# A feed-forward layer's gate and up products as seven half-size products in place of eight

## The chip, the cores and the metric

The kernel runs on one core of a Trainium2 chip. The metric is the device time of one execution in microseconds (us). Three runs of the kernel before took 2739.49, 2741.16 and 2741.25 us; the median is 2741.16 us. The engines are named as in the profile: PE is TensorE's matmul, PEld its load of the stationary operand, DVE is VectorE, ACT is ScalarE, POOL is GpSimd, and SP issues the transfers (DMAs).

## The reference

It is one decoder block on 512 tokens, with a width of 2048 and an inner width of 5632, in float32. An attention part and a pooling part are mixed, projected and added to x. The change lies behind that, in the gated feed-forward:

```python
        x = x + mixed @ w_out[l]

        h2 = rmsnorm(x, ffn_norm_g[l])
        x = x + (jax.nn.silu(h2 @ w_ffn_gate[l]) * (h2 @ w_ffn_up[l])) @ w_ffn_down[l]
```

## The kernel before, in words

Everything is kept feature-major: a tile is 128 features on the partitions and 512 tokens along the columns. The weights are the stationary operand (128 x 128), the activations stream past them. To keep float32's precision each operand x is split into h = float32r(x) and l = float32r(x - h), and each product becomes three matmuls that add up in one bank of PSUM (`mm3`, L192): h.h, h.l, l.h. `split` (L168) makes h with a cast on ACT and l with a subtraction on DVE that reads x and h.

Each stage is a list of items for PE. `Program.emit` (L97) issues them in order and puts the loads and splits of the weights ahead of them: three raw buffers of 128 x 1024 (`raw`), which SP fills with 512 KB each, and five split buffers (`wsp`) of 512 columns. PE's order is the order written; on the other engines a scheduler orders the instructions.

`gemm` (L199) computes four column tiles at once, in four banks, over all row tiles. The stages around the change are these. The output projection has four such groups (L990); their `post` (L999) adds x, keeps x2 in SBUF and sums its squares. Then the inner width is walked in four chunks of 6, 6, 6 and 4 groups (L1033). A group (L1056) multiplies two column tiles of gate and two of up by the 16 tiles of the normed x2 (`make_h2`, L1008), that is 16 x 4 x 3 = 192 matmuls of 512 columns; its `post` (L1044) multiplies by the norm's factor for each token (`inv2_bc`), applies Silu, multiplies gate by up, and splits the result. Behind each chunk the down projection adds its part onto x2 (L1060). The last chunk stores the result.

Two pieces of other stages serve as a measure of the change's operations. The attention's projections (`k_item`, `v_item`, L737 and L764) have matmuls of 256 columns, and the norms of the attention's heads run on POOL (`norm_chain`, L656, and L760).

Of the kernel before, what the change touches and what calls it, by code (L numbers as in the profile page):

```python
# [10 lines left out]

# [13 lines left out]
NT = S // 128  # L25
# [5 lines left out]
FF_CHUNKS = (6, 6, 6, 4)  # L31
# [9 lines left out]
RAW_BUFS, WSP_BUFS = 3, 5  # L41
WARM = 8
# [3 lines left out]
class Unit:  # L46
    """A stretch of weights that one DMA brings: n columns of float32 per partition, used in pieces."""
# [19 lines left out]
class Step:  # L67
    """Work other than a piece's that an item needs done ahead of it."""
# [5 lines left out]
class Program:  # L74
    """Tensor-engine items in issue order; the weights of later items are split ahead of them."""
# [4 lines left out]
    def item(self, run, pieces=(), post=(), pre=()):  # L80
        """post: (delay in items, function); pre: (lead in items, function)"""
# [48 lines left out]
def hybrid_block(ctx, tc, xT, pos, wcq, wckv, wkr, wu, wgp, wga, wgrp, wpo, wq, wkv, wao, wo,  # L130
                 wgu, wdn, vec, rgain, ident_d, mask_d, freq_d, cnt_d, out):
# [6 lines left out]
    stage = ctx.enter_context(tc.tile_pool(name="stage", bufs=1))  # L138
    work = ctx.enter_context(tc.tile_pool(name="work", bufs=1))
    dram = ctx.enter_context(tc.tile_pool(name="dram", bufs=1, space=bass.MemoryType.DRAM))  # L140
    psum = ctx.enter_context(tc.tile_pool(name="psum", bufs=2, space=bass.MemoryType.PSUM))
    SETS = ("aacc", "bbcd")
# [25 lines left out]
    def split(hi, lo, src, scale=None):  # L168
        """hi + lo = src (times a factor per partition), hi on ScalarE, lo on VectorE."""
# [22 lines left out]
    def mm3(o, w_h, w_l, a_h, a_l, start, stop):  # L192
        pe.matmul(o, w_h, a_h, start=start, stop=False)  # L193
        pe.matmul(o, w_h, a_l, start=False, stop=False)  # L194
        pe.matmul(o, w_l, a_h, start=False, stop=stop)  # L195
# [60 lines left out]
    def units_of(w, g, n):  # L256
        return [w[g, u] for u in range(n)]

# [1 line left out]
    vecs = small([128, N_VEC])  # L260
    nc.sync.dma_start(vecs, vec)
    ident = small([128, 128])
# [881 lines left out]
```

## Time and profile before

| | |
|---|---|
| median of 3 runs | 2741.16 us |
| span of the profiled execution | 2739.4 us |
| profiled execution's own device time | not given apart from its span; the three runs lie 0.1 to 1.9 us above it |
| PE busy | 2729.4 us, 100% of the span, 12712 matmuls |
| PEld busy | 2279.0 us |
| DVE, ACT, POOL busy | 1189.2, 940.0, 102.0 us |
| first matmul of gate and up | 1297.42 us after the span's start |
| DMA | 295.51 MB, mean 108 GB/s |

A group's row has the line, the engine, the operation, the output and the inputs by the program's names (buffer numbers left out), partitions x columns and the count; after the bar the busy time in us and the mean duration of one in ns, and after the next bar the idle time of the engine ahead of it and what ended it. A row of the timeline begins with the start and the duration in us. Matmuls overlap in the pipeline, so that the distance between two starts, not the duration, is what one costs. L-numbers are lines of the kernel that the row belongs to; those of the changed kernel are its own.

### The profile page before, as it was taken

To read this page: it belongs to the slowest core of one execution; us is meant where nothing else is said; L and a number is where in the kernel's file an instruction comes from. 1 tells how busy PE (TensorE), PEld (TensorE's weight loads), DVE (VectorE), ACT (ScalarE), POOL (GpSimd) and SP (SyncE) were. 2 spreads that over 40 slices of the span, in tenths; PEclk is the share of its full clock that TensorE was granted. 3 is DMA by queue.
4 is the path that set the end of the run, shared out by engine and by line. 5 is a ranking of instruction groups with operands and counts; after the bars stand their busy time and mean duration, and the time that the engine had idled before them with its cause. 6 is when DMAs were issued, how large, how long until landed. Compare 5 with 4: busy or idle time off the path is not lost.

```text
span 2739.4 us, 32926 instructions
## 1 busy us (share of the span) xinstructions
PE 2729.4 (100%) x12712; PEld 2279.0 (83%) x12712; DVE 1189.2 (43%) x2372; ACT 940.0 (34%) x1924; POOL 102.0 (4%) x232
## 2 busy tenths in 40 slices
PE   9999999999999999999999999999999999999999
PEld 7888888888888888888888888888888888888887
DVE  6555323367777644344333333333332333333343
ACT  5223223366667432233222322223222222222231
POOL 0000000021323000000000000000000000000000
PEclk9999999999999999999999999999999999999999
DMA  5223333322222554342232232322323222232233
GB/s 181 85 93 115 122 120 128 112 89 85 93 89 82 190 164 151 119 141 98 93 100 95 98 100 92 100 94 99 99 94 100 94 99 97 96 100 93 100 94 121
DMA packets 95085, 295.51 MB, mean 108 GB/s; under 512 B 10832, under 2 KB 11216, under 8 KB 94928
## 3 DMA queue, kind: packets, MB, share of 16 engines
q1 hardware_dynamic: 94928, 293.41, 32.6%
q8 instruction: 99, 1.62, 0.2%
q14 instruction: 58, 0.48, 0.1%
HBM read 272.40 MB, written 20.97 MB: 107 GB/s over the span
## 4 chain that ended last, share of the span: by engine, by line
PE 99%; DMA 0%; ACT 0%; SPq 0%; DVE 0%; issue 0%
PE psc L194 11%; PE psc L193 11%; PE psc L195 11%; PE psa L193 9%; PE psa L194 9%; PE psa L195 9%; PE psb L193 8%; PE psb L194 8%; PE psb L195 8%; PE psd L193 5%; PE psd L195 5%; PE psd L194 5%; PE psb L791 1%; PE psc L822 1%; PE psc L697 1%; PE psb L790 0%
## 5 line engine op out<-in xcount | busy, mean ns | idle before, releaser
L172 DVE TENSOR_TENSOR wsp<-raw,wsp 128x512 fp32r<-128x512 f32 (+1 forms) x954 | 649.7, 684 | 1413.3 <-ACT wsp L171 1410.9
L171 ACT CAST wsp<-raw 128x512 fp32r<-128x512 f32 (+1 forms) x954 | 587.7, 617 | 1612.5 <-PE psd L195 798.2
L195 PE MATMUL psc<-h,wsp 128*128 128x512 f32 x528 | 205.4, 389 | 0.0
L193 PE MATMUL psc<-h,wsp 128*128 128x512 f32 x528 | 205.4, 389 | 0.0
L194 PE MATMUL psc<-h,wsp 128*128 128x512 f32 x528 | 205.4, 389 | 0.0
L193 PE MATMUL psa<-h,wsp 128*128 128x512 f32 x352 | 137.4, 390 | 0.0
L195 PE MATMUL psa<-h,wsp 128*128 128x512 f32 x352 | 137.0, 389 | 0.0
L194 PE MATMUL psa<-h,wsp 128*128 128x512 f32 x352 | 136.9, 389 | 0.0
L193 PE MATMUL psb<-h,wsp 128*128 128x512 f32 x352 | 136.9, 389 | 0.0
L194 PE MATMUL psb<-h,wsp 128*128 128x512 f32 x352 | 136.9, 389 | 0.0
L195 PE MATMUL psb<-h,wsp 128*128 128x512 f32 x352 | 136.9, 389 | 0.0
L193 PE MATMUL psa<-wsp,lr 128*128 128x256 f32 (+1 forms) x384 | 120.9, 315 | 1.0 <-ACT pt L758 1.0
L194 PEld LDWEIGHTS psc<-h,wsp 128*128 128x128 f32 x528 | 99.1, 188 | 20.7
L195 PEld LDWEIGHTS psc<-h,wsp 128*128 128x128 f32 x528 | 99.1, 188 | 20.6
L193 PEld LDWEIGHTS psc<-h,wsp 128*128 128x128 f32 x528 | 99.0, 188 | 20.5
L195 PE MATMUL psa<-wsp,lr 128*128 128x256 f32 (+1 forms) x384 | 115.4, 300 | 0.0
L194 PE MATMUL psa<-wsp,lr 128*128 128x256 f32 (+1 forms) x384 | 115.3, 300 | 0.0
L193 PE MATMUL psc<-hT,wsp 128*128 128x512 f32 x288 | 112.6, 391 | 0.0
L195 PE MATMUL psc<-hT,wsp 128*128 128x512 f32 x288 | 112.6, 391 | 0.0
L194 PE MATMUL psc<-hT,wsp 128*128 128x512 f32 x288 | 112.5, 391 | 0.0
L193 PE MATMUL psc<-ff,wsp 128*128 128x512 f32 x264 | 102.7, 389 | 0.0
L194 PE MATMUL psc<-ff,wsp 128*128 128x512 f32 x264 | 102.7, 389 | 0.0
(309 smaller groups left out, 5619.8 us busy)
## 6 DMA issues: line engine op xcount, KB each, us to landing
raw<-in_wgu SPq DMA_DIRECT2D x176, 512.0 KB, 3.3
raw<-in_wdn SPq DMA_DIRECT2D x88, 512.0 KB, 3.3
raw<-in_wgp SPq DMA_DIRECT2D x32, 512.0 KB, 3.3
raw<-in_wga SPq DMA_DIRECT2D x32, 512.0 KB, 3.4
raw<-in_wao SPq DMA_DIRECT2D x32, 512.0 KB, 3.5
raw<-in_wo SPq DMA_DIRECT2D x32, 512.0 KB, 3.3
raw<-in_wu SPq DMA_DIRECT2D x16, 512.0 KB, 3.4
G_d<-tmp SPq DMA_DIRECT2D x32, 256.0 KB, 2.8
```

Of the source, the lines that this page charges most:

```text
L171: act.copy(out=hi, in_=src)
L172: dve.tensor_tensor(out=lo, in0=src, in1=hi.bitcast(F32), op=ALU.subtract)
L193: pe.matmul(o, w_h, a_h, start=start, stop=False)
L194: pe.matmul(o, w_h, a_l, start=False, stop=False)
L195: pe.matmul(o, w_l, a_h, start=False, stop=stop)
L697: pe.transpose(box[0][:, j * 128:(j + 1) * 128], src[t][:, j * 128:(j + 1) * 128], ident)
L791: pe.matmul(s[:, :w], P.QR[hp, h, q], P.KL[hp, :w], start=False, stop=True)
L822: pe.transpose(box[0][:, j * 128:(j + 1) * 128], P.st[h, i][:, j * 128:(j + 1) * 128], ident)
```

## The change

Gate and up are taken as one product of a 2 x 2 block matrix of weights and a 2 x 2 block matrix of activations. The weights' blocks are named by output (1 gate, 2 up) and half of the input width; so 11 and 12 are gate's halves, 21 and 22 up's. The activations' blocks are the same halves of the width by halves of the tokens (256 columns). A form of Strassen's identity (Winograd's) gets the four result blocks from seven block products in place of eight, with sums of blocks ahead of the products and behind them.

The activations' sums are made once, in the output projection (`operands`): for each pair of row tiles seven operands, split into h and l side by side, `T[i, j]`. The weights' sums are made for each of the 44 tiles of the inner width, in a class called `Macro`. A macro loads four blocks of 128 x 1024, makes four sums (two on POOL, two on DVE), splits seven operands of 1024 columns, and issues seven products of 8 x 3 matmuls with 256 columns, in the order 1, 6, 2, 7, 5, 4, 3. Product 2 adds onto product 1's bank. `post` adds the products up, applies the norm's factor (partly on POOL) and Silu, and stores the tile to DRAM (`F_d`).

The down projection runs after all macros, in two halves of 22 inner tiles, and reads its operands back from `F_d` (`make_act`). x2 goes to DRAM (`X2_d`), as does the sum after the first half (`X3_d`). The buffers of the three parts (ahead of the macros, macros, down) lie in pools that are closed and opened between the parts, in the same memory. The item list is emitted in two programs, with the macros between them.

```diff
-FF_CHUNKS = (6, 6, 6, 4)
+FT = D_FF // 128
+HT = FT // 2
+RAW2_BUFS, WS_BUFS = 6, 3
...
+        def sums():
+            t, b = box["t"], box["b"]
+            d, e = slot(F32, "d"), slot(F32, "e")
+            t1, t2, t3, t4 = d[:, :, LO], d[:, :, HI], e[:, :, LO], e[:, :, HI]
+            dve.tensor_tensor(out=t1, in0=t[:, :, HI], in1=t[:, :, LO], op=ALU.subtract)
+            dve.tensor_tensor(out=t2, in0=b[:, :, HI], in1=t1, op=ALU.subtract)
+            dve.tensor_tensor(out=t3, in0=b[:, :, HI], in1=t[:, :, HI], op=ALU.subtract)
+            dve.tensor_tensor(out=t4, in0=t2, in1=b[:, :, LO], op=ALU.subtract)
+            box.update({1: t[:, :, LO], 2: b[:, :, LO], 3: b[:, :, HI], 4: t4, 5: t1, 6: t2, 7: t3})
...
+    ORDER = (1, 6, 2, 7, 5, 4, 3)
+    TAGS = {1: "a", 6: "b", 7: "c", 5: "c", 4: "b", 3: "d"}
+    LEAD = 2
...
+        def split(self, i, src):
+            r = fast.tile([128, 2, 1024], F32R, name="ws", tag="ws", bufs=WS_BUFS)
+            split(r[:, 0, :], r[:, 1, :], src)
+            self.s[i] = r
+
+        def prepare(self, i):
+            raw = self.raw
+            if i == 1:
+                self.split(1, raw["11"])
+            elif i == 6:
+                self.s3 = fast.tile([128, 1024], F32, name="s3", tag="raw", bufs=RAW2_BUFS)
+                pool.tensor_tensor(out=self.s3, in0=raw["11"], in1=raw["21"], op=ALU.subtract)
+                pool.tensor_tensor(out=raw["21"], in0=raw["21"], in1=raw["22"], op=ALU.add)
+                dve.tensor_tensor(out=raw["11"], in0=raw["21"], in1=raw["11"], op=ALU.subtract)
+                self.split(6, raw["11"])
+            elif i == 2:
+                self.split(2, raw["12"])
+            elif i == 7:
+                self.split(7, self.s3)
+            elif i == 5:
+                self.split(5, raw["21"])
+            elif i == 4:
+                self.split(4, raw["22"])
+            else:
+                dve.tensor_tensor(out=raw["12"], in0=raw["12"], in1=raw["11"], op=ALU.subtract)
+                self.split(3, raw["12"])
+
+        def product(self, i):
+            if i == 2:
+                o = self.ps[1]
+            else:
+                o = self.ps[i] = ps(TAGS[i])[:, LO]
+            s = self.s[i]
+            for k in range(HK):
+                c = slice(k * 128, (k + 1) * 128)
+                t = T[i, k // 2][:, k % 2, :]
+                mm3(o, s[:, 0, c], s[:, 1, c], t[:, LO], t[:, HI], k == 0 and i != 2, k == HK - 1, onto=i == 2)
...
+            elif i == 4:
+                dve.tensor_tensor(out=self.gu[:, 1, LO], in0=self.u3, in1=o, op=ALU.subtract)
+                pool.tensor_tensor(out=self.gu[:, 1, :], in0=self.gu[:, 1, :], in1=inv2_bc, op=ALU.mult)
+            else:
+                g = self.gu
+                dve.tensor_tensor(out=g[:, 0, HI], in0=o, in1=self.u4, op=ALU.add)
+                pool.tensor_tensor(out=g[:, 0, HI], in0=g[:, 0, HI], in1=inv2_bc[:, HI], op=ALU.mult)
+                act.activation(out=g[:, 0, :], in_=g[:, 0, :], func=AF.Silu)
+                dve.tensor_tensor(out=g[:, 1, :], in0=g[:, 0, :], in1=g[:, 1, :], op=ALU.mult)
+                nc.sync.dma_start(F_d[self.f], g[:, 1, :])
```

How the instructions stand in the built programs follows here at three places. First DVE in the steady part of gate and up. Before, `post` of a group (`tmp`, `ff`) stands among splits of 512 columns:

```order
L172 TENSOR_TENSOR wsp<-raw,wsp 128x512 x16
L1049 TENSOR_TENSOR tmp<-psa,bc 128x512
L1051 TENSOR_TENSOR tmp<-psc,bc 128x512
L1049 TENSOR_TENSOR tmp<-psa,bc 128x512
L1052 TENSOR_TENSOR tmp<-tmp 128x512
L1051 TENSOR_TENSOR tmp<-psc,bc 128x512
```

Now DVE goes through one macro like this, from the split of product 3 to the first split for the next product 2 (`ws` are split buffers, `raw` the weights' blocks, `u` and `gu` the sums behind the products; `raw_15185` is this macro's block 12, `raw_15187` and `raw_15226` are the next one's blocks 11 and 21):

```order
L180 TENSOR_TENSOR ws_15348<-raw_15185,ws_15348 128x1024
L1160 TENSOR_TENSOR u_15376<-psc_15351,u_15286 128x256
L1161 TENSOR_TENSOR gu_15315<-psc_15351,u_15345 128x256
L180 TENSOR_TENSOR ws_15381<-raw_15187,ws_15381 128x1024
L1116 TENSOR_TENSOR raw_15187<-raw_15226,raw_15187 128x1024
L1163 TENSOR_TENSOR gu_15315<-u_15345,psb_15384 128x256
L180 TENSOR_TENSOR ws_15419<-raw_15187,ws_15419 128x1024
L1167 TENSOR_TENSOR gu_15315<-psd_15422,u_15376 128x256
L180 TENSOR_TENSOR ws_15454<-raw_15411,ws_15454 128x1024
```

The subtraction L1116 stands in DVE's queue ahead of the sum L1163 and of the splits of products 6 and 2; it reads what POOL has made.

POOL was idle in this part before, but for one operation of 4 columns. Its queue now, over the same macro (`s3` is the difference of 11 and 21, in a buffer of the raw ones):

```order
L1114 TENSOR_TENSOR s3_15415<-raw_15187,raw_15226 128x1024
L1115 TENSOR_TENSOR raw_15226<-raw_15226,raw_15379 128x1024
L1164 TENSOR_TENSOR gu_15315<-gu_15315,bc_111 128x512
L1168 TENSOR_TENSOR gu_15315<-gu_15315,bc_111 128x256
L1114 TENSOR_TENSOR s3_15641<-raw_15413,raw_15452 128x1024
```

The first of these waits for the split `ws_15348` of product 3, which frees its buffer; that split's cast waits for the last matmul of product 7. The second waits for the first.

Last, DVE where the output projection ends. Before, behind the last sum of x and x2 (L1001, `psd`) stood the squares and the splits of the normed x2, among splits of the weights:

```order
L1001 TENSOR_TENSOR x_11162<-psd,x_11162 128x512
L320 TENSOR_TENSOR s<-s,tmp 128x512
L172 TENSOR_TENSOR wsp<-raw,wsp 128x512
L320 TENSOR_TENSOR s<-s,tmp 128x512
L175 SCALAR_TENSOR_TENSOR h_11653<-x_11160,k_74,h_11653 128x512
```

Now the last group's sums and seven splits (`T`) stand there, and only then the first split of a macro's weights; ahead of these rows are the last sums of x and x2, the squares and the products with the norm's gain:

```order
L1020 TENSOR_TENSOR d_11542<-y_11536 128x2x256
L1022 TENSOR_TENSOR e_11543<-y_11539,y_11536 128x2x256
L1021 TENSOR_TENSOR d_11542<-y_11539,d_11542 128x2x256
L180 TENSOR_TENSOR T_11548<-y_11536,T_11548 128x2x256
L1023 TENSOR_TENSOR e_11543<-d_11542,y_11539 128x2x256
L180 TENSOR_TENSOR T_11551<-d_11542,T_11551 128x2x256
L180 TENSOR_TENSOR T_11554<-y_11539,T_11554 128x2x256
L180 TENSOR_TENSOR T_11557<-e_11543,T_11557 128x2x256
L180 TENSOR_TENSOR T_11560<-d_11542,T_11560 128x2x256
L180 TENSOR_TENSOR T_11563<-e_11543,T_11563 128x2x256
L180 TENSOR_TENSOR T_11566<-y_11539,T_11566 128x2x256
L180 TENSOR_TENSOR ws_11580<-raw_11574,ws_11580 128x1024
```

The macro's first split has moved behind all of the last group's operands, where before the weights' splits stood between them.

More of the change, by code (lines that the diff above doesn't have):

```diff
@@ L10 @@
 import math
+from contextlib import ExitStack
 import concourse.bass as bass
@@ L190, in split_piece, with mm3 @@
             split(p.t[:, 0, :p.n], p.t[:, 1, :p.n], raw)
[L192 to L195, printed above, removed]
+    def mm3(o, w_h, w_l, a_h, a_l, start, stop, onto=False):
+        for w, a, first, last in ((w_h, a_h, start, False), (w_h, a_l, False, False), (w_l, a_h, False, stop)):
+            pe.matmul(o, w, a, start=first, stop=last, skip_group_check=onto)
     prog = Program()
@@ L1073, in _turns @@
+    prog.emit(load_unit, split_piece, lambda load_next: None)
+    phase.close()
 def _turns(k):
```

235 lines of the change are left out of this document (164 added, 71 removed).

## The prediction

> **What bounds the kernel now.** I read the page's totals and its chain of waits first, then the table of stretches, then single rows.
>
> ```profile
> span 2739.4 us, 32926 instructions
> PE 2729.4 (100%) x12712; PEld 2279.0 (83%) x12712; DVE 1189.2 (43%) x2372; ACT 940.0 (34%) x1924; POOL 102.0 (4%) x232
> PE 99%; DMA 0%; ACT 0%; SPq 0%; DVE 0%; issue 0%
> ```
>
> TensorE (PE) is the bound: its matmuls fill the span and 99% of the chain. The stretches say whether this also holds where the change lies, in the feed-forward part (its first matmul starts at 1297.42, in a row below):
>
> ```profile
> core 0: us, PE busy (x) PEld busy (x) DVE busy (x) ACT busy (x) POOL busy (x), PEclk, DMA share, GB/s
> 1130.00:1305.00 175.00, 175.00 (x774) 144.91 (x773) 73.20 (x113) 57.93 (x97) 0.00 (x0) 1.00 0.35 116
> 1305.00:1600.00 295.00, 295.00 (x1305) 244.01 (x1304) 107.96 (x168) 83.11 (x133) 1.03 (x1) 1.00 0.30 97
> 1600.00:2000.00 400.00, 400.00 (x1767) 331.20 (x1766) 139.80 (x212) 106.35 (x171) 0.00 (x0) 1.00 0.30 96
> ```
>
> PE is busy for all of each stretch at full clock, while DVE (VectorE) and ACT (ScalarE) work a third of it, POOL (GpSimd) nearly nothing and the DMA engines 30%. So any matmul time saved here shows, as long as none of these others takes over. A busy PE isn't a rate, so the price of a matmul is the distance between starts:
>
> ```profile
> 2000.14 0.39 PE L195 MATMUL psc<-ff,wsp 128*128 128x512 f32 x1
> 2005.13 0.39 PE L193 MATMUL psc<-ff,wsp 128*128 128x512 f32 x1
> ...
> 626.86 0.28 PE L193 MATMUL psa<-wsp,lr 128*128 128x256 f32 x1
> 628.17 0.28 PE L195 MATMUL psa<-wsp,lr 128*128 128x256 f32 x1
> ```
>
> There are 22 distances between the first two rows (4.99 us): 0.2268 us for 512 columns. There are 11 between the last two (1.31 us): 0.119 us for 256 columns, each with weights of its own as in the change. Half the columns cost 5% more than half.
>
> **The matmuls.** Gate and up are 22 groups x 16 row tiles x 4 columns x 3 = 4224 matmuls of 512 columns: 4224 x 0.2268 = 958.0 us. The change has 44 macros x 7 products x 8 row tiles x 3 = 7392 of 256 columns: 7392 x 0.119 = 879.6 us. That is **-78 us**, not the eighth (-120 us) that the arithmetic promises. The down projection keeps its 2112 matmuls. A macro is 168 matmuls, 20.0 us, a product 2.86 us; a 44th part of gate and up was 21.8 us, so a stall of **1.8 us per macro** eats the gain.
>
> **What must be ready for a macro.** The sums of weights and the splits into high and low half move from 512 to 1024 columns and to more engines. Prices:
>
> ```profile
> L172 DVE TENSOR_TENSOR wsp<-raw,wsp 128x512 fp32r<-128x512 f32 x914 | 629.2, 690 | 1398.3 <-ACT wsp L171 1396.3
> L172 DVE TENSOR_TENSOR PT<-psc,PT 128x256 fp32r<-128x256 f32 x64 | 26.2, 419 | 24.1 <-ACT PT L171 24.1
> ...
> L171 ACT CAST wsp<-raw 128x512 fp32r<-128x512 f32 x914 | 568.0, 623 | 1594.4 <-PE psd L195 792.5 <-PE psc L195 772.3 <-issue 8.8
> L171 ACT CAST PT<-psc 128x256 fp32r<-128x256 f32 x64 | 23.8, 373 | 9.7 <-DVE PT L172 9.2 <-PE psc L822 0.5
> L1050 ACT ACTIVATE tmp<-tmp 128x512 f32<-128x512 f32 x44 | 27.9, 633 | 29.4 <-DVE tmp L1049 29.3
> ```
>
> 256 columns more cost DVE 271 ns and ACT 250 ns, so 1024 columns cost 690 + 2 x 271 = 1.23 us and 623 + 2 x 250 = 1.12 us. Per macro DVE has 9 of these (11.1 us), a product of 512 columns (0.69) and 8 sums of 256 (3.4): 15 us. ACT has 7 casts, a copy and a Silu: 8.9 us. Neither is the bound by itself. POOL gets two sums of 1024 columns and products of 512 and 256. Nothing like it stands in the trace; the nearest rows are small ones (minimum, median and maximum in ns):
>
> ```profile
> L658 POOL TENSOR_TENSOR ss<-ss,k x40: 194/195/554, 540.9 to 889.6; 128x2 f32<-128x2 f32 x32, 128x8 f32<-128x8 f32 x8
> L760 POOL TENSOR_SCALAR rt<-k,inv x64: 442/449/942, 546.1 to 892.2; 128x64 f32<-128x64 f32 x64
> ```
>
> (449 - 195) / 62 = 4.1 ns per column puts 1024 columns at 4.2 us, the dear end; the cheap end is DVE's 1.23 us for the same operation. I take the geometric middle, **2.3 us**, since the nearest POOL rows differ in operation and size. The Trainium skill (GPSIMD Engine Reference, 3.1) gives 4497 ns for such a sum over 2048 columns, which would make it about 2.25 us as an estimate from that page; no run here shows it.
>
> **Who shares with whom.** The long maxima in these rows have one cause, in this stretch of POOL and of DVE:
>
> ```profile
> 602.18 0.19 POOL L659 TENSOR_TENSOR ss<-ss,k 128x2 f32<-128x2 f32 x1
> 610.06 0.20 POOL L658 TENSOR_TENSOR ss<-ss,k 128x2 f32<-128x2 f32 x1 [2.58 <-ACT tmp L749]
> 614.34 0.47 POOL L658 TENSOR_TENSOR ss<-ss,k 128x2 f32<-128x2 f32 x1 [1.89 <-ACT tmp L749]
> 614.89 0.52 POOL L659 TENSOR_TENSOR ss<-ss,k 128x2 f32<-128x2 f32 x1
> ...
> 602.13 0.42 DVE L172 TENSOR_TENSOR PT<-psc,PT 128x256 fp32r<-128x256 f32 x1 [0.75 <-ACT PT L171]
> 614.08 1.28 DVE L172 TENSOR_TENSOR wsp<-raw,wsp 128x512 fp32r<-128x512 f32 x2
> ```
>
> Alone or beside a DVE operation that reads PSUM, POOL's op takes 0.19 to 0.20 us. Beside the two DVE subtractions with both inputs in SBUF it takes 0.47 and 0.52 us, and ends at 614.81 and 615.41: 0.05 us after the first subtraction (614.08 + 0.68) and after the pair (615.36). POOL stands still while DVE reads two SBUF operands. In the change DVE does this for 11.8 us of every macro, and POOL needs 2 x 2.3 + 1.2 + 0.6 = 6.4 us: 18 us of 20 that can't overlap.
>
> The Trainium skill (SBUF — State Buffer, "Who interferes with whom") says more than the rows: whichever starts first holds the port for its whole instruction and the other fully blocks. By that, DVE also waits out POOL's 2.3 us sums, worth a few us more over the span than if only POOL waits; the rows bear out one direction alone, since no POOL op here is long enough to hold DVE up.
>
> **The chain of a macro.** POOL's first sum (`s3`) needs a raw buffer, and the order of the program gives it the one that product 3's split frees. That split needs the split buffer that product 7 leaves. From product 7's end: last matmul's drain 0.16 (0.28 - 0.12), ACT cast 1.12, DVE split 1.23, POOL sum 2.3, the split for the next product 1, which sits between POOL's two sums on the shared reads, 1.23, POOL sum 2.3, DVE's subtraction that waits for it 1.23, ACT cast 1.12, DVE split behind POOL's product with the norm factor 0.4 + 1.23, and eight handoffs of 0.05 (0.08 from 614.81 to 614.89 on POOL): 12.7 us. There are four products (5, 4, 3 and the next 1), 11.4 us, until product 6 starts, plus 0.24 until its third matmul reads the low half: 11.7 us. It is **1.0 us late**.
>
> To that come a weight load that nothing hides, 0.19 us (the 188 ns below), and a knock-on between nothing and the Silu's 0.63 us, of which I take 0.4: product 2 adds onto product 1's bank and waits until ACT has copied it, and this copy stands behind the Silu, which waits for POOL's last product. 1.65 us x 43 = **+71 us**.
>
> ```profile
> L195 PEld LDWEIGHTS psc<-h,wsp 128*128 128x128 f32 x528 | 99.1, 188 | 20.6
> ```
>
> The stall's bounds: nothing at a POOL price under 1.8 us, or at 2.3 us if DVE's split didn't stand in the way (12.7 - 1.23 - 0.4 = 11.1 us); at 4.2 us the chain is 3.8 us longer and POOL's product some 0.5, 6 us per macro, +258 us.
>
> **The two seams.** Before, the output projection runs into the feed-forward without a gap:
>
> ```profile
> 1297.19 0.39 PE L195 MATMUL psd<-mixT,wsp 128*128 128x512 f32 x1
> 1297.42 0.39 PE L193 MATMUL psa<-h,wsp 128*128 128x512 f32 x1
> ...
> 1297.37 0.68 DVE L1001 TENSOR_TENSOR x<-psc,x 128x512 f32<-128x512 f32 x1
> 1297.96 0.68 DVE L320 TENSOR_TENSOR s<-s,tmp 128x512 f32<-128x512 f32 x1
> ...
> raw<-in_wgu SPq DMA_DIRECT2D x176, 512.0 KB, 3.3
> ```
>
> Now the weights' loads (3.3 us) stand on SP behind stores of x2 that wait for DVE, and some 17 DVE instructions for the last group of operands stand before the first macro's low half: 17 x 0.59 (the distance of the two DVE rows) + 1.23 = 11 us, and up to two POOL sums in between, 16 us. I take **+16**, as the rows above show such reads excluding each other. At the end of the macros the loads for down stand behind the last store of the product: drain 0.16, DVE 0.42, POOL 0.6, Silu 0.63, DVE 0.69, load 3.3, cast 0.62, handoffs: 7 us; with the splits of the first inner tiles queued on DVE and ACT ahead of these, up to 13. I take **+11**.
>
> The other operand groups (22 DVE instructions each, 13 us) lie in quarters of the output projection in which DVE is 42% busy (73.20 of 175); uncovered they would cost 3 x 13 us. The inner product's way through DRAM adds 88 transfers of 256 KB to queues at 30%: nothing.
>
> **Sum.** -78 + 71 + 16 + 11 = **+20 us**, onto the profiled execution's span of 2739.4; with the 1.8 us by which the median (2741.16) exceeds that span, **2761 us**. By the POOL price alone the case reaches from 2744 (2.1 us) to 2815 (2.8 us).
>
> **Rivals.**
> Macros without stall (0.38): POOL's sum costs under 1.8 us, or reads beside DVE when it streams long rows. For it: the rows show exclusion on ops of two columns only, and PE, DVE and ACT sums all stay below 20 us. Against: 18 of 20 us on one resource, in fixed order. -78 + 16 + 11 = -51: **2690 us**, at the cheap ends of the seams 2681.
> POOL as dear as its TENSOR_SCALAR row (0.05): 4.2 us a sum, stall 6 us per macro, slower from 2.1 us a sum on: -78 + 258 + 27 = +207, **2948 us**. Against it: that row has a scalar operand and a start-up of its own.
> Matmuls of 256 columns held to the 188 ns of a weight load: 7392 x 0.188 = 1390 us, +432, about 3173 us. The rows at 0.119 speak against it; under 0.01.
>
> **Numbers.** The forecast's case has 0.57: 0.50 slower and 0.07 where the stall is near 1.2 us and all cancels. 0.2% is 5.5 us, about what a measurement here can tell from no change. Faster 0.38, same 0.07, slower 0.50 + 0.05 = 0.55. The range runs from 2684 (no stall, seams near cheap) to 2830 (POOL near 3 us).
>
> **What would show it.** Right: in the macros PE waits for DVE's split of product 6 by about 1 us and for ACT's copy by a few tenths, POOL's 1024-column rows last over 2.3 us because DVE's reads hold them, macros come every 21 to 22 us, and PE pauses 10 to 20 us at each seam. Wrong: POOL's sums under 1.8 us, or macros every 20.0 us with PE waiting for nothing.

## The result and the profile after

The changed kernel takes 2775.17 us (median of 4 runs, 2772.37 to 2780.71), the kernel before 2740.67 beside it (2739.49 to 2741.25): a ratio of 1.0129, 95% interval 1.0114 to 1.0143. It is 1.3% slower; 2761 us had been forecast, in a range of 2684 to 2830. The profiled execution took 2773.10 us with a span of 2771.3.

The page's totals and its chain of waits, after:

```profile
span 2771.3 us, 40184 instructions
PE 2697.8 (97%) x15880; PEld 2393.0 (86%) x15880; DVE 1533.7 (55%) x2648; ACT 1046.6 (38%) x1936; POOL 483.9 (17%) x408
PE 18%; issue 1%; POOL 1%; ACT 1%; DMA 1%; DVE 0%; POOLq 0%; ACTq 0%; SPq 0%
```

PE's busy time fell only from 2729.4 to 2697.8 us, and 73.5 us of the span are now free of matmuls; before it was 10. The chain could be followed for a small part alone, so its shares say little here. The table of stretches says more:

```profile
core 0: us, PE busy (x) PEld busy (x) DVE busy (x) ACT busy (x) POOL busy (x), PEclk, DMA share, GB/s
900.00:1280.00 380.00, 379.55 (x1689) 313.09 (x1688) 185.04 (x320) 128.30 (x228) 0.00 (x0) 1.00 0.47 154
1280.00:1320.00 40.00, 25.37 (x112) 21.72 (x111) 20.86 (x30) 11.14 (x17) 8.85 (x2) 0.76 0.28 102
1320.00:1545.00 225.00, 206.76 (x1590) 201.93 (x1589) 153.47 (x174) 80.20 (x93) 78.36 (x37) 0.94 0.33 110
1545.00:2200.00 655.00, 636.35 (x5175) 623.77 (x5174) 456.53 (x524) 244.43 (x278) 267.15 (x124) 1.00 0.33 111
2200.00:2290.00 90.00, 75.85 (x604) 73.95 (x604) 73.01 (x94) 44.50 (x63) 28.55 (x14) 0.93 0.51 178
```

Ahead of the feed-forward PE is as full as before. At the first seam (1280 to 1320) it stands idle for 15 us of 40, and at the second (2200 to 2290) for 14 of 90. In the macros between them it waits a little in each. Two stretches of macros differ: up to 1545 PE is idle 8% of the time and the granted clock is 0.94; behind that it is 3% and 1.00.

The macros' stores of the inner product give their period: 24.24 us in the mean for the first eight intervals (193.9 us), 21.24 for the other 35 (743.5 us), most of them 21.27. The rows of one steady macro, PE first, then POOL and DVE (start, duration, and in brackets what ended the wait ahead):

```profile
1703.44 0.40 PE L203 MATMUL psb<-T,ws 128*128 128x256 f32 x2
1704.35 2.90 PE L203 MATMUL psb<-T,ws 128*128 128x256 f32 x22 [0.51 <-DVE ws L180]
1707.34 3.13 PE L203 MATMUL psa<-T,ws 128*128 128x256 f32 x24
1710.30 5.92 PE L203 MATMUL psc<-T,ws 128*128 128x256 f32 x48
1716.06 3.04 PE L203 MATMUL psb<-T,ws 128*128 128x256 f32 x24
1718.94 3.04 PE L203 MATMUL psd<-T,ws 128*128 128x256 f32 x24
...
1701.92 1.29 POOL L1164 TENSOR_TENSOR gu<-gu,bc 128x512 f32<-128x512 f32 x1 [1.67 <-DVE gu L1163]
1715.77 2.40 POOL L1114 TENSOR_TENSOR s<-raw 128x1024 f32<-128x1024 f32 x1 [9.41 <-DVE ws L180]
1718.25 3.27 POOL L1115 TENSOR_TENSOR raw<-raw 128x1024 f32<-128x1024 f32 x1
...
1702.70 1.59 DVE L180 TENSOR_TENSOR ws<-raw,ws 128x1024 fp32r<-128x1024 f32 x1 [0.86 <-ACT ws L179]
1710.27 1.21 DVE L180 TENSOR_TENSOR ws<-raw,ws 128x1024 fp32r<-128x1024 f32 x1
1717.35 1.90 DVE L180 TENSOR_TENSOR ws<-raw,ws 128x1024 fp32r<-128x1024 f32 x1 [0.33 <-ACT ws L179]
1721.55 1.23 DVE L1116 TENSOR_TENSOR raw<-raw 128x1024 f32<-128x1024 f32 x1 [2.29 <-POOL raw L1115]
```

Undisturbed products start 2.88 us apart (1716.06 to 1718.94): 0.120 us for a matmul, 20.16 us for the 168 of a macro. The 22 matmuls of product 6 (`psb`, 1704.35) start 0.67 us later than 1703.44 + 2 x 0.12, product 2 (1707.34) 0.35 later than their 22 x 0.12 allow, product 7 (1710.30) another 0.08. That is the stall of 1.10 us.

POOL's first sum takes 2.40 us though DVE's split starts beside it, as long as a sum with nothing beside it (2.37 at 1309.31, below). The DVE split that starts at 1717.35 takes 1.90 where others take 1.21: nearly all of its work lies behind POOL's end at 1718.17, and POOL's next sum, issued at 1718.25, in turn takes 0.87 more than 2.40. So DVE waits for POOL as POOL waits for DVE. The forecast's rows showed only the second; the rule of the Trainium skill (SBUF — State Buffer, "Who interferes with whom") that whichever starts first holds the port is borne out in both directions.

In the first eight intervals something else is added. The rows are ACT in the second of them, with one cast of the steady macro (1713.38) for comparison, then PE at the end of the first and of the second, and then the granted clock over the 22 matmuls of product 6 in both:

```profile
1375.66 0.62 ACT L179 CAST ff<-ff 128x512 fp32r<-128x512 f32 x1 [3.01 <-DMA ff<-F_d]
1376.18 2.23 ACT L179 CAST ws<-raw 128x1024 fp32r<-128x1024 f32 x2
...
1713.38 1.05 ACT L179 CAST ws<-raw 128x1024 fp32r<-128x1024 f32 x1 [1.83 <-PE psc L203]
...
1364.30 4.19 PE L203 MATMUL psb<-T,ws 128*128 128x256 f32 x22 [1.11 <-DVE ws L180]
1386.78 0.50 PE L203 MATMUL psb<-T,ws 128*128 128x256 f32 x2 [0.82 <-ACT ws L179]
1388.39 4.35 PE L203 MATMUL psb<-T,ws 128*128 128x256 f32 x22 [1.11 <-DVE ws L180]
1392.54 0.73 PE L203 MATMUL psa<-T,ws 128*128 128x256 f32 x4
```

```profile
1364.30:1368.29 3.99, 3.99 (x22) 3.99 (x23) 2.71 (x4) 1.83 (x3) 1.64 (x1) 0.64 0.00 0
1388.39:1392.54 4.15, 4.15 (x23) 4.15 (x23) 2.87 (x4) 1.83 (x3) 1.64 (x1) 0.61 0.00 2
```

The eight early reloads of the inner product (`ff<-F_d`), written for the last four macros, stand in the queues of the first eight: nothing held them back, since their buffers were free. Each is issued behind the store that it reads; its cast stands in ACT's queue and waits 3.01 us for it to land, and the casts of two weight splits stand behind it. The first of these belongs to product 3, whose split lets POOL's first sum begin. It starts 4.78 us behind product 7's start (1376.18, product 7 at 1371.40), in the steady macro 3.08 (1713.38 and 1710.30): 1.70 us later. Product 6's low half comes 2.35 us late in place of 0.67, 1.68 more. PE's waits there are 0.82 and 1.11 us, and then the granted clock drops: 22 matmuls take 4.15 us from start to start in place of 2.64. One wait of 0.51 us, in the steady macro, costs its length; these two cost 1.5 us more.

The seams, PE and POOL:

```profile
1293.85 0.84 PE L203 MATMUL psd<-mixT,wsp 128*128 128x512 f32 x3
1305.30 0.79 PE L203 MATMUL psa<-T,ws 128*128 128x256 f32 x2 [10.61 <-ACT ws L179]
1307.05 4.53 PE L203 MATMUL psa<-T,ws 128*128 128x256 f32 x22 [0.96 <-DVE ws L180]
1314.12 0.73 PE L203 MATMUL psb<-T,ws 128*128 128x256 f32 x2 [2.54 <-ACT ws L179]
1315.38 5.06 PE L203 MATMUL psb<-T,ws 128*128 128x256 f32 x22 [0.53 <-DVE ws L180]
1321.43 1.79 PE L203 MATMUL psa<-T,ws 128*128 128x256 f32 x13
2286.78 3.05 PE L203 MATMUL psa<-ff,wsp 128*128 128x512 f32 x6 [12.95 <-ACT wsp L179]
...
1302.74 6.49 POOL L1114 TENSOR_TENSOR s<-raw 128x1024 f32<-128x1024 f32 x1 [412.95 <-DMA raw<-in_wup]
1309.31 2.37 POOL L1115 TENSOR_TENSOR raw<-raw 128x1024 f32<-128x1024 f32 x1
```

POOL's first sum lasts 6.49 us under DVE's row of operand splits. The whole difference of the spans (31.9 us) then comes out like this:

| part | predicted | measured | how |
|---|---|---|---|
| matmuls of gate and up | -78 | -71.0 | 44 x 20.16 - 958.0 |
| eight intervals with a reload | 0 | +32.6 | 8 x (24.24 - 20.16) |
| the other 35 intervals | +71 with the eight | +37.9 | 743.5 - 35 x 20.16 |
| both seams' gaps | +27 | +34.7 | 2286.78 - 1294.53, less 937.4 between the first store and the last, less one macro |
| slow clock behind the second seam | 0 | +1.5 | six matmuls in 3.05 us, 1.52 elsewhere |
| part ahead | 0 | -2.9 | output projection ends at 1294.53 (1293.85 + 3 x 0.227), before at 1297.42 |
| sum | +20 | +32.8 | |

The first seam is 21 us of the 34.7 (1321.43 - 1294.53 - 2 x 2.88). Of the 32.6 us, 8 x 1.11 = 8.9 are the stall that the other intervals have too, and 23.8 are left for the reloads. The end of the output projection varies between runs by as much (it lies at 1297.70 in the run below with the operands behind the splits), so no cause is read from the -2.9 of the part ahead. About 1 us of the sum stays unassigned.

### The profile page after: what moved, and what is told of

It is laid out like the page before. It is cut to its first block, busy times and chain, and to the rows that moved or that the text cites. A ratio compares the mean times of both kernels' runs of the same rounds, so it can differ in the third digit from the quotient of the medians.

```text
span 2771.3 us, 40184 instructions
## 1 busy us (share of the span) xinstructions
PE 2697.8 (97%) x15880; PEld 2393.0 (86%) x15880; DVE 1533.7 (55%) x2648; ACT 1046.6 (38%) x1936; POOL 483.9 (17%) x408
## 5 line engine op out<-in xcount | busy, mean ns | idle before, releaser
L180 DVE TENSOR_TENSOR wsp<-raw,wsp 128x512 fp32r<-128x512 f32 (+1 forms) x602 | 406.2, 679 | 796.2 <-ACT wsp L179 791.8
L179 ACT CAST wsp<-raw 128x512 fp32r<-128x512 f32 (+1 forms) x602 | 368.3, 614 | 939.0 <-PE psd L203 456.7
L179 ACT CAST ws<-raw 128x1024 fp32r<-128x1024 f32 x264 | 272.4, 1049 | 459.2 <-DVE raw L1116 252.0
L180 DVE TENSOR_TENSOR ws<-raw,ws 128x1024 fp32r<-128x1024 f32 x264 | 377.8, 1431 | 77.7 <-ACT ws L179 77.5
L203 PE MATMUL psb<-T,ws 128*128 128x256 f32 x2112 | 291.7, 293 | 37.9 <-DVE ws L180 26.2
L203 PEld LDWEIGHTS psb<-T,ws 128*128 128x128 f32 x2112 | 273.3, 199 | 48.9 <-DVE ws L180 35.2
L203 PE MATMUL psa<-T,ws 128*128 128x256 f32 x2112 | 274.4, 286 | 14.9 <-ACT ws L179 10.6
L203 PEld LDWEIGHTS psa<-T,ws 128*128 128x128 f32 x2112 | 261.6, 193 | 23.3 <-ACT ws L179 11.0
L203 PE MATMUL psc<-T,ws 128*128 128x256 f32 x2112 | 260.6, 283 | 0.0
L203 PEld LDWEIGHTS psc<-T,ws 128*128 128x128 f32 x2112 | 256.6, 192 | 0.0
```

The costliest lines, as they stand in the source:

```text
L179: act.copy(out=hi, in_=src)
L180: dve.tensor_tensor(out=lo, in0=src, in1=hi.bitcast(F32), op=ALU.subtract)
L203: pe.matmul(o, w, a, start=first, stop=last, skip_group_check=onto)
```

## The experiments

All times are medians of at least 4 runs; the kernel before took 2740.1 to 2740.6 us beside them. A steady period is that of macros 10 to 37.

| edit to the changed kernel | steady period, us | time, us | ratio to before, interval |
|---|---|---|---|
| none | 21.27 | 2775.17 | 1.0129, 1.0114 to 1.0143 |
| sums on DVE | 20.16 | 2711.75 | 0.9896, 0.9882 to 0.9911 |
| reloads late | 21.27 | 2757.61 | 1.0063, 1.0048 to 1.0078 |
| both | 20.16 | 2706.07 | 0.9875, 0.9860 to 0.9890 |
| reloads late, both norm products on DVE | 20.56 | 2722.68 | 0.9941, 0.9924 to 0.9957 |
| reloads late, norm product of 512 columns on DVE | 20.90 | 2743.02 | 1.0009, 1.0000 to 1.0018 |
| reloads late, own buffer for the first sum | 19.8 to 20.95 | 2726.78 | 0.9947, 0.9932 to 0.9961 |
| both, down's weights early | 20.16 | 2691.67 | 0.9822, 0.9806 to 0.9839 |
| the same, operands behind the splits | 20.16 | 2691.68 | 0.9819, 0.9804 to 0.9834 |
| reloads late, chain longer by one operation | 21.84 | 2777.04 | 1.0135, 1.0118 to 1.0152 |
| reloads late, chain longer by two | 24.6 to 25.8 | 2888.12 | 1.0538, 1.0522 to 1.0554 |
| both, down's weights early, reloads one at a time | 20.16 | 2693.04 | 0.9827, 0.9812 to 0.9842 |
| the same, POOL idle | 20.16 | 2688.28 | 0.9811, 0.9794 to 0.9827 |

**Sums on DVE.**

```diff
-                pool.tensor_tensor(out=self.s3, in0=raw["11"], in1=raw["21"], op=ALU.subtract)
-                pool.tensor_tensor(out=raw["21"], in0=raw["21"], in1=raw["22"], op=ALU.add)
+                dve.tensor_tensor(out=self.s3, in0=raw["11"], in1=raw["21"], op=ALU.subtract)
+                dve.tensor_tensor(out=raw["21"], in0=raw["21"], in1=raw["22"], op=ALU.add)
```

> The two weight sums of a macro, 128 x 1024, go from POOL to DVE; the two products with the norm's factor stay on POOL. In the changed kernel a steady macro comes every 21.27 us, where its 168 matmuls alone need 168 x 0.120 = 20.16; the first nine come every 24.15. Theory A (POOL's sums, 2.40 alone and 3.27 us when DVE's reads hold them, make the macro late): DVE does each in 1.22 us, the chain loses 2.40 + 3.27 - 2 x 1.22 = 3.2 us and no longer waits, so steady macros come every 20.2 us, and the first nine too if the same chain sets them: 2775 - 37 - 36 = about 2702 us. If the first nine have a cause of their own (theory B: eight early reloads of the inner product stand in SP's queue ahead of the weights' loads), they stay at 23 to 24 us and the time is about 2738. Theory B for every macro (SP's queue with its store and loads sets the period): nothing changes, 2770 to 2778, or slower, as DVE gets 2.4 us more work per macro.

Measured 2711.75 us, 63 less. The steady period is 20.16: the chain without POOL's sums no longer reaches PE. The eight intervals with a reload take 21.1 us in the mean, so the reloads still cost about 1 us each, where 0 or 3 had been expected; with room in the chain they cost less, not nothing. (The expectation speaks of nine such macros; the stores show eight.)

**Reloads late.** Eight tiny copies keep the eight buffers taken until four macros before the end.

```diff
+        if i == 1 and m.f == 1:
+            pads = [slot(F32, "pad") for _ in range(8)]
+        if i == 1 and m.f in (1, FT - 4):
+            for r in pads:
+                dve.tensor_copy(r[:, 0, 0:1], m.raw["22"][:, 0:1])
```

> The eight reloads of the inner product that the scheduler had placed among the first eight macros (each behind the store that it reads, ahead of the next weights' loads in SP's queue) are held back until four macros before the end, by eight tiny copies that keep their buffers taken; sums stay on POOL. Theory B (the reloads delay the weights in the first nine macros): their period falls from 24.15 to the steady 21.3 us, 9 x 2.9 = 26 us, and the time to about 2749; the steady macros keep 21.27. Theory A alone (POOL's chain, made longer there by the granted clock of 0.91 to 0.95 and by the doubled DMA traffic): the first nine stay at 23.5 us or more and the time within 2768 to 2778.

Measured 2757.61 us. The early periods are 21.27 (the first 20.97), so the reloads were the whole difference of the eight intervals: 8 x (24.24 - 21.27) = 23.8 us. But the macros where they now stand took 26.66 and 21.82, which gives 5.9 back: 17.9 us are left, and 17.6 were measured. The expectation put the cause into SP's queue ahead of the weights' loads. SP's rows in the changed kernel, with a reload and without, don't show that:

```profile
1367.71 0.33 SPq L1171 DMA_DIRECT2D F_d<-gu  x1
1370.40 0.42 SPq L1087 DMA_DIRECT2D ff<-F_d  x1
1371.49 2.77 SPq L1100 DMA_DIRECT2D raw<-in_wg  x2
...
1707.78 0.33 SPq L1171 DMA_DIRECT2D F_d<-gu  x1
1711.55 1.76 SPq L1100 DMA_DIRECT2D raw<-in_wg  x2
```

From the store to the loads of gate it is 3.78 us in the one and 3.77 in the other. The second of the two loads is issued about 1 us later with a reload, but no operation between 1340 and 1545 waits for a load of weights: the waits for transfers there are the eight casts of reloads, 27.0 us, and one of 1.3 us for a store. The place that the rows show is ACT's queue, as above; no run moved the cast alone, so it is read from rows, not tried.

**Both.** The two edits together.

> Both edits: sums on DVE and reloads late. Theory A for the steady macros and B for the first nine, added up: every macro at 20.2 us, 2775 - 73 = about 2702 us, of which only the two seams (15 and 13 us) are left as gaps of PE; -71 + 28 against the kernel before = about 2698. If DVE, now with some 17.6 us of work in 20.2, becomes late itself (theory C: the work was moved, not removed), macros come at 20.5 to 21.5 us and the time is 2715 to 2760.

Measured 2706.07 us: 34.1 less than before, where 2702 had been expected by the sum of the theories. PE is busy in every microsecond from 1500 to 1800. DVE is 83% busy there (249 us of 300) and PE doesn't wait for it, so the theory that the work was only moved falls. POOL still makes its two products under DVE's reads:

```profile
1718.18 2.16 POOL L1164 TENSOR_TENSOR gu<-gu,bc 128x512 f32<-128x512 f32 x1 [17.24 <-DVE gu L1163]
1720.36 0.74 POOL L1168 TENSOR_TENSOR gu<-gu,bc 128x256 f32<-128x256 f32 x1
```

2.16 us in place of 1.29, and it costs nothing, since the chain ends early enough.

**Both norm products on DVE, then one.** The sums stay on POOL; the reloads are late.

```diff
-                pool.tensor_tensor(out=self.gu[:, 1, :], in0=self.gu[:, 1, :], in1=inv2_bc, op=ALU.mult)
+                dve.tensor_tensor(out=self.gu[:, 1, :], in0=self.gu[:, 1, :], in1=inv2_bc, op=ALU.mult)
...
-                pool.tensor_tensor(out=g[:, 0, HI], in0=g[:, 0, HI], in1=inv2_bc[:, HI], op=ALU.mult)
+                dve.tensor_tensor(out=g[:, 0, HI], in0=g[:, 0, HI], in1=inv2_bc[:, HI], op=ALU.mult)
```

> As the run with the late reloads, and the two products with the norm's factor (512 columns 1.29 us, 256 columns 1.65 us held by DVE's reads) go from POOL to DVE; the weight sums stay on POOL. If the sums' chain alone sets the period (theory A, sums), the steady period stays near 21.3 us, or gains only the 0.4 to 0.7 us by which POOL's 512-column product holds up DVE's split of product 6: 0 to 25 us less than with the late reloads alone. If the knock-on through Silu and product 1's copy is what PE waits for (theory A, knock-on: 0.53 us before product 2's later matmuls), it goes and PE's wait at product 6 (0.4 to 0.5 us) stays or shrinks: 15 to 37 us less.

Measured 2722.68 us, period 20.56: 34.9 us less than with the late reloads alone, more than the sums' theory allows (25), for two operations of 2.9 us on an engine that is 17% busy. The second run moves the first of the two alone:

> As the run with the late reloads, and of the two products with the norm's factor only the one of 512 columns goes to DVE; the one of 256 columns stays on POOL. Moving both shortened the period from 21.27 to 20.56 us. In the run with the late reloads a macro's 1.10 us of stall falls into 0.67 at product 6's third matmul, 0.35 ahead of product 2 and 0.08 ahead of product 7. Theory A1 (POOL's product of 512 columns holds DVE's split of product 6: that split took 1.59 in place of 1.22 us): 0.36 us goes at product 6, and the 0.43 ahead of products 2 and 7 stays, since Silu still waits for POOL's product of 256 columns (1.65 us): period 20.9, time about 2742. Theory A2 (all of it hangs on product 6): period 20.56, time about 2726. Theory A3 (all of it hangs on the way through Silu and the copy of product 1): period 21.27, 2757.

Measured 2743.02 us, period 20.90. Theory A1 holds (20.9 and 2742 had been expected): 0.37 us a macro is the hold on product 6's split, and the remaining 0.34 the way through Silu to product 1's copy. Of the steady stall of 1.11 us the two small products make 0.71, and 0.40 is left to the sums when these are gone. Taking the sums away ends the whole stall as well, because all of this stands in one chain: what each is worth depends on what was taken away before.

**Own buffer for the first sum.**

```diff
-                self.s3 = fast.tile([128, 1024], F32, name="s3", tag="raw", bufs=RAW2_BUFS)
+                self.s3 = s3_own[self.f % 2]
...
+    s3_own = [slot(F32, "s3").rearrange("p a n -> p (a n)") for _ in range(2)]
```

> As the run with the late reloads, and the first weight sum goes into two buffers of its own (taken from the 8 held ones) in place of the buffer that product 3's split frees. Both sums and both products stay on POOL at their price. Theory A as predicted (the price counts because the chain starts at that split: POOL waits 9.4 us for it in every macro): POOL's two sums begin as soon as the loads of up have landed, products earlier, DVE's subtraction no longer waits 2.3 us for them, and macros come every 20.2 to 20.6 us: 2757 - 43 x 0.7 to 1.1 = 2710 to 2727. Theory D (what counts is the shared reads themselves, 18 of 20 us that can't overlap, wherever they begin): period stays at 21.0 to 21.3 us, 2745 to 2757.

Measured 2726.78 us, 30.8 less than with the late reloads alone. (Two of the eight held buffers serve for it.) POOL does the same work, only earlier; it is no cheaper there, the product of 512 columns even takes 2.27 us in the mean in place of 1.29. Its waits show the change of what releases it:

```profile
POOL s L1114 <- DMA raw<-in_wup: 587.3, 32, 412.9
POOL raw L1115 <- DMA raw<-in_wup: 266.5, 42, 7.2
```

It waits for the weights' loads in most macros, and in none for product 3's split. So it is the place in the chain that counts, not the 18 us of shared reads as such (theory D falls). What remains of the stall, up to 0.8 us, comes where POOL's sum now happens to meet a split: in one such macro product 6's split took 2.92 us.

**Down's weights early.** Three blocks and the first four splits of the down projection go into buffers outside of the macros' memory. Five tiles of the inner product are reloaded early for it, in place of eight.

```diff
+        if m.f == FT - 2 and i == 5:
+            for u in range(3):
+                r = slot(F32, "early").rearrange("p a n -> p (a n)")
+                nc.sync.dma_start(r, wdn[0, u].rearrange("p a n -> p (a n)"))
+                early.append(r)
...
+    def split_down(p):
+        nsplit[0] += 1
+        if nsplit[0] > 4:
+            split_piece(p)
+        else:
+            p.t = slot(F32R, "wsp0")
+            split(p.t[:, 0, :p.n], p.t[:, 1, :p.n], p.unit.raw[:, p.off:p.off + p.n])
```

> As the run with sums on DVE and late reloads, and the seam to the down projection changed: three weight blocks of down are loaded before the last macro ends, into buffers that no macro uses, and the first four splits go into such buffers too; five tiles of the inner product are reloaded early in place of eight. If the 13 us that PE waits there come from loads and splits that wait for the macros' memory, behind the last store and the reloads' splits, the gap falls to 0 to 3 us: 2706 - 10 to 13 = about 2694. If they come from the last macro's own way through Silu and store, or from the reloads' splits on DVE (22 x 0.60 us), the gap stays at 9 to 13 us: 2702 to 2706.

Measured 2691.67 us, 14.4 less than with both edits. The seam is gone:

```profile
2203.83 3.04 PE L203 MATMUL psd<-T,ws 128*128 128x256 f32 x24
2206.71 1.55 PE L203 MATMUL psa<-ff,wsp 128*128 128x512 f32 x6
```

The first matmul of down starts 2.88 us after the last product, as if it were one more product. In the run with both edits 12.96 us of wait and 1.4 of slow clock (2.93 us for down's first six matmuls in place of 1.52) had stood there: 14.4.

**Operands behind the splits.** At the first seam only product 1's operand is made ahead of the macros.

```diff
-                    for f in steps:
+                    for f in steps[:4]:
                         f()
+                    late.extend(steps[4:])
...
             mm.prepare(ii)
+            if mm.f == 0 and late:
+                late.pop(0)()
```

> As the run with down's weights early, and at the first seam only product 1's operand of the last group is made ahead of the macros; the other six stand behind the first splits of weights, one behind each. If the order sets this seam (the first split waits for seven operands' splits), PE starts 3 to 6 us earlier and keeps it: 2688 to 2691. If DVE's amount of work sets it (about 24 us from the last x2 to product 7's operands in either order), PE starts 2 to 4 us earlier and gives it back ahead of product 6: within 1.5 us of the run without this.

Measured 2691.68 us, the same. PE's first wait falls from 10.62 to 8.54 us and a part comes back ahead of product 6 (1.72 in place of 1.41); from the output projection's end to product 2 it is 22.7 us in place of 24.1. So the order is worth 1.5 us at most, which these times can't show. This is what had been expected if DVE's amount of work sets the seam, but no run made that work less, so the cause isn't shown. It is the one gap that no edit here closed.

**A longer chain.** One or two operations on DVE (block 21 times 1.0, in place) between POOL's second sum and DVE's subtraction, in macros 3 to 37.

```diff
+                if 3 <= self.f < FT - 6:
+                    for _ in range(2):
+                        dve.tensor_scalar(out=raw["21"], in0=raw["21"], scalar1=1.0, scalar2=None, op0=ALU.mult)
```

> As the run with the late reloads, and between POOL's second sum and DVE's subtraction stands one more operation on DVE in macros 3 to 37: block 21 times 1.0 in place, 1024 columns, 0.6 to 0.9 us by the row of 512 columns (0.48 us). It makes the chain of a macro that much later. In that run PE's wait for product 6 is 0.51 us and the granted clock stays at 1.00; in the changed kernel's first nine macros PE waits 0.82 and 1.11 us and the clock behind that is 0.61 over 4.1 us. Theory linear (a wait costs its length): period 21.27 + 0.6 to 0.9 = 21.9 to 22.2, 2757 + 35 x 0.6 to 0.9 = 2778 to 2789. Theory clock (a wait of about 2 us in product 6 also halves the granted clock for 3 to 4 us, 1.3 us or more on top): not reached yet with one wait of 1.1 to 1.4 us, so the same 2778 to 2789 with the clock at 1.00; if it is reached, period 23.2 to 23.8 and 2825 to 2845.

> As the run before, with two such operations in place of one: the chain is 1.2 to 1.8 us later than with the late reloads alone. Theory linear: period 22.5 to 23.1 us, 2757 + 35 x 1.2 to 1.8 = 2799 to 2820, granted clock 1.00 throughout. Theory clock: PE waits 1.7 us or more for product 6, the granted clock falls to about 0.5 to 0.7 over the 4 us behind it in most macros, the period is 23.8 to 24.8 and the time 2845 to 2880.

One operation costs 0.61 us on DVE (0.69 by its row) and lengthens the period by 0.57, to 21.84: 2777.04 us, linear, with the clock at 1.00. Two make 24.6 to 25.8 us: 2888.12, above even the clock theory's range. PE in such a macro, and the stretch of the 22 matmuls:

```profile
1704.19 3.04 PE L203 MATMUL psa<-T,ws 128*128 128x256 f32 x24
1708.99 0.50 PE L203 MATMUL psb<-T,ws 128*128 128x256 f32 x2 [1.75 <-ACT ws L179]
1710.24 4.32 PE L203 MATMUL psb<-T,ws 128*128 128x256 f32 x22 [0.76 <-DVE ws L180]
1714.40 3.04 PE L203 MATMUL psa<-T,ws 128*128 128x256 f32 x24
```

```profile
1710.24:1714.40 4.16, 4.16 (x23) 4.16 (x23) 3.96 (x4) 1.38 (x3) 0.00 (x0) 0.61 0.30 81
```

PE is late by 1.92 and 1.01 us, and the clock of 0.61 adds 1.52 (4.16 less 2.64). Together that is 4.45 us; the period is 4.44 over 20.16. That the waits grew by more than the added operation has a second cause in the rows: DVE's subtraction now takes 2.19 us in place of 1.22, as POOL's product of 512 columns has come to stand beside it.

**Reloads one at a time, then POOL idle.** The held buffers are freed where each reload stands.

```diff
-            make_act(2 * (m.f - FT + 4) + (i == 5))
+            n_act = 2 * (m.f - FT + 4) + (i == 5)
+            dve.tensor_copy(pads[n_act][:, 0, 0:1], m.raw["22"][:, 0:1])
+            make_act(n_act)
```

> As the run with down's weights early, but the held buffers are freed one at a time, where each reload stands in the program, in place of all eight at once four macros before the end. There two macros took 22.57 and 23.55 us in place of 20.16, 5.8 us together, with six casts of reloads in a row on ACT ahead of a split (3.79 us) in the run with both edits. If that heap is the cost: 2692 - 4 to 6 = about 2687. If the reloads' own work on DVE and ACT (0.60 and 0.52 us each) costs that wherever it stands: 2690 to 2694.

Measured 2693.04 us, no gain. The heap of casts was not the cost; three intervals took 21.22, 23.07 and 21.32 us. The dearest had this on DVE and POOL:

```profile
2166.65 1.79 DVE L180 TENSOR_TENSOR ff<-ff 128x512 fp32r<-128x512 f32 x1
...
2165.73 2.16 POOL L1164 TENSOR_TENSOR gu<-gu,bc 128x512 f32<-128x512 f32 x1 [16.26 <-DMA early<-in_wdn]
```

The reload's split, 0.60 us elsewhere, stands ahead of product 6's and is held by POOL. PE then waits 1.51 us, and the granted clock is 0.60 over the 22 matmuls behind that, which take 4.25 us. The last run puts both norm products on DVE as well:

> As the run with reloads freed one at a time, and the two products with the norm's factor on DVE too, so that POOL does nothing in the macros. In that run freeing them singly gained nothing: the macros around the reloads still took 21.22, 23.07 and 21.32 us, 5.1 over three times 20.16, and in the dearest of them DVE's split of a reload stood ahead of product 6's split for 1.79 us in place of 0.60, since POOL's product of 512 columns held it. Theory lock (that hold is the cost of the reloads): without POOL the three macros take 20.2 to 20.6 each, 2693 - 3 to 5 = 2688 to 2690. Theory work (DVE has no room for the reloads' splits: 18.7 us of 20.16 in a macro now): they stay at 21 us or more, 2692 to 2696.

Measured 2688.28 us, 4.8 less. PE has no gap any more from 1340 to 2215, where down has begun (its first matmul starts at 2202.72):

```profile
1340.00:2100.00 760.00, 760.00 (x6335) 760.00 (x6335) 643.42 (x792) 302.63 (x338) 0.00 (x0) 1.00 0.37 119
2100.00:2215.00 115.00, 115.00 (x913) 112.88 (x912) 105.11 (x151) 63.03 (x86) 0.00 (x0) 1.00 0.54 183
```

DVE works 643 of 760 us (85%) and carries the reloads too, so the lack of room on DVE was not it. (One store interval there is still 22.82 us, but PE doesn't wait in it.) This version beats the kernel before by 1.9% and the changed one by 3.1%: 2740.46 - 71 for the matmuls + 18.7 for its first seam (1320.53 - 1296.05 - 2 x 2.88) is 2688.2.

## Why the prediction was right, and where it was not

**The side was right**, for the reason given: the matmuls save less than an eighth, and a chain over DVE, POOL and ACT that ends at product 6's low half costs PE 47 us (43 x 1.10) of the 71 that they save; the seams cost more than the rest. With the reloads late the kernel is still slower than before, at 2757.61 us. The first rival's condition, a sum under 1.8 us, did not hold: it costs 2.40. Its time (2690) is reached only with the stalls and the second seam cured (2691.67, with POOL idle 2688.28).

**Matmuls, -78.** Measured -71: 0.120 us where 0.119 had been taken from 11 distances, which is 7 us over 7392 matmuls. The sum was mis-sized by one in the third digit.

**The chain of a macro, 12.7 us.** From product 7's end (1713.18) to the 22 matmuls of product 6 (1725.62 in the same macro's count, 1704.35 + 21.27) it took 12.4. Its parts: sum 2.40 (taken 2.3), cast 1.05 (1.12), split 1.21 (1.23), hold by the norm product 0.37 (0.4), and DVE's split between POOL's sums just where it had been put. The two-sided lock, which had been left to the Trainium skill alone, belongs to it. The sum had it in without a row for it: the split stands there in full behind POOL's sum. Without it DVE's split at 1717.35 would have ended at 1718.56, 0.7 us earlier, and POOL's second sum with it. The lateness is 0.67 (1.0 had been said), the weight load that nothing hides (0.19) does not show on top, and the knock-on is 0.43 (0.4). So the stall is 1.10, not 1.65 us, from a chain that was right to 0.3 us: where the difference of two long chains sets the cost, 2% of a chain is nearly half of the lateness.

**The way through DRAM: "nothing".** This step failed. It looked at the queues' share, 30%, and not at where the eight reloads and their casts would be placed. They cost 23.8 us beyond the stall, a third of all that the macros lose, since their casts hold up the cast of product 3's split in ACT's queue by 1.70 us. By chance this made up for the stall's excess, 43 x 0.55 = 23.7: 71 predicted, 70.5 measured, out of other parts.

**What was not in it: the clock.** That PE's waits also lower the granted clock was left out. It is part of the eight intervals (1.4 and 1.5 us in the two shown; 23.9 us at half clock over all eight, which is up to 12 us) and of both seams.

**First seam, +16.** 21: the waits up to product 1's low half were foreseen (10.61 and 0.96 us, 11 said), and so was a POOL sum held by DVE's reads (6.49 us). Up to product 6's low half it is 17.7 us. Not foreseen was that the products then run at half the clock: product 6's 22 matmuls take 4.85 us in place of 2.64 (1315.38 to 1320.23), and eight small matmuls behind them 1.2. Product 1's run slowly too (1307.05), but a wait of 2.54 us stands behind them all the same. **Second seam, +11, bounds 7 to 13.** 13 and 1.5 for the clock. The splits that were to stand in front on DVE and ACT did: product 3's last sum starts on DVE at 2278.10, behind five splits of reloads. The run with down's weights early shows that the wait was for down's loads and splits. Since these were moved both ahead of the last store and into memory of their own, it doesn't separate the place in the queue from the macros' memory.

**The price of POOL's sum.** 2.3 from the middle of two far bounds against 2.40 measured; the estimate from the Trainium skill (GPSIMD Engine Reference, 3.1), 2.25, was about as near.

**The times by POOL's price.** The forecast's 2815 us at 2.8 us a sum doesn't follow from its own terms: two sums in 43 macros add 43 us for half a microsecond, with the share of POOL's product some 49, which is 2804 to 2810.

## What to carry to other kernels

A helper engine that is 17% busy can set the time: ask in whose chain its operations stand and what they lock out, not how long it works. When an edit frees a buffer or takes a wait away, ask what the scheduler will now put early, and which in-order queue will stand behind it. A chain that is late by a microsecond is cheap to cure by starting it earlier (a buffer of its own gained 30.8 us, taking 2.9 us of work off the engine 34.9), and worth curing before waits grow to two.

## What the hardware showed that was not expected

Waits of PE have a price that is not linear. Waits of 0.51, 0.76 and 1.08 us alone left the granted clock at 1.00; 0.82 and 1.11 us within 2.4 us brought it to half for 3.4 us (0.61 over 4.15), 1.75 with 0.76 did so again (0.61 in the macro shown, 0.90 to 0.91 over all these macros), and so did 1.51 us nearly alone (0.60 over 4.25, reloads one at a time). Not all pairs did: one with 1.78 and 1.11 us (at 1532) kept 1.00.

The traces show more. In every run the clock changes on a fixed grid: each stretch of half clock, but for those at the ends of the run, lasts 3.41 us or a multiple of it. In the changed kernel's macros the windows of this grid ahead of such a stretch hold 9 to 14 matmuls, where some 28 would fit, with PE busy for 1.31 to 1.65 us. The window with the wait of 1.08 us holds 20, and the clock stayed. The pair at 1532 is cut by a window's edge at 1532.67, and its two windows hold 15 and 17. So it seems to count how full a window is, with a limit near half of it; the exact limit stays open, as PE was busy for 1.63 us in the window of 15, no more than in some of those that halved the clock.

The Trainium skill (TensorE: Matmul & The Clock Gate, "Part 1: The HAM clock gate") gives half the rate after an idle window of about 3.4 us and a window that runs free of the kernel. The half rate and the window's length agree with the traces; but here less than 2 us of waits, with matmuls between them, were enough.

The lock between DVE's operations with two operands in SBUF and POOL's works in both directions and by whole instructions: 1.90 us for a split of 1.21 that came 0.82 us before POOL's end, 3.27 for a sum of 2.40 that came behind it, and 6.49 us for a sum beside seven splits.
